# A pool of its own for the streamed matmul operands, at the upper end of on-chip memory

## The chip, the cores and the metric

The kernel runs on one core of one Trainium2 chip. The metric is the device time of one execution in microseconds (us); the lower the better. A core has a tensor engine (PE, with its weight loads shown apart as PEld), a vector engine (DVE), a scalar engine (ACT), GpSimd (POOL) and a synchronisation engine (SP) that here issues most of the transfers. Its on-chip memory has 128 partitions; in this program's allocation tiles lie between byte 16,384 and byte 229,376 of each partition.

## The reference

A sequence of 512 tokens with 1024 features goes through two blocks in float32.

```python
h = rms_norm(x, norm1_g);  z = h @ w_in
mix = concat([pool_mixer, gated short convolution, gated long convolution, differential attention])
x = x + mix @ w_out
h2 = rms_norm(x, norm2_g)
x = x + (silu(h2 @ w_gate) * (h2 @ w_up)) @ w_down
```

The second block puts 16 meta tokens in front and has two layers, each `h = h + layer(rms_norm_2(h, g))`: layer ab (sparse attention with a learned choice of keys, and a gated linear attention in chunks) and layer cd (a retention in chunks and a stick-breaking attention). A last norm ends it.

## The kernel before

Everything is kept transposed: features on the partitions, tokens along the free dimension. The activations are 8 tiles (kt) of 128 features by T = 528 columns, 16 meta tokens and 512 tokens. To reach float32 accuracy with faster matmuls, each operand is split into a high part and a low part (hi and lo) of the type float32r; a product is then three matmuls, hi by hi, lo by hi and hi by lo.

The work is staged as `run` (line 1342) has it: `setup`, `layer1` (line 394), `ffn` (646), `layer_ab` (772), `layer_cd` (1225). Each stage has a pool of its own ("l1", "ffn", "ab", "cd") that is closed at its end, so that the next stage's pool takes the same addresses; with `reuse_waits="tile"` a tile waits only for those earlier tiles that lay where it lies.

Three pools live through the whole kernel: "const" (line 63), "big" (64) and "w" (65). The pool "big" holds, among others, the residual x; `mx` (line 266, four tiles of 2 x 528 columns, 4,224 bytes each), in which mixed channels stand as hi and lo; and `hhi` and `hlo` (line 213, eight tiles each of 528 columns, 2,112 bytes), the hi and lo parts of the activations that `feed` (209) makes for each kt. The last stage also keeps its output weights in hhi and hlo (line 126). The pool "w" holds raw weights (`wraw`, two tiles of 4,096 bytes) and their parts (`whi`, `wlo`, four tiles each of 512 columns, 2,048 bytes).

`weights` (108) issues a weight load on SP's queue, casts it on ACT to hi (line 129) and subtracts on DVE to lo (line 130). `f_acc` (136) is the loop of nearly all matmuls: for each part of the contraction it issues three at line 144.

```python
for i, (ah, al) in enumerate(act):
    for j, (ww, aa) in enumerate(((wh, ah), (wh, al), (wl, ah))):
        nc.tensor.matmul(ps[b], lhsT=ww[i][:, f0:f0 + nf], rhs=aa[:, t0:t1], ...)
```

The operand `rhs` is streamed past the loaded weights. In layer 1 and in the gate and up projections of the FFN it is columns 16 to 528 of hhi and hlo; in the FFN's down projection it is `hidh` and `hidl` (lines 664 and 665, 13 tiles each of 512 columns, 2,048 bytes); in `add_out` (274) it is mx; in layers ab and cd it is mostly hhi and hlo in two parts of 272 and 256 columns. The FFN has two halves; each makes 11 tiles of hid by 22 products of 24 matmuls and then 8 outputs of 33 matmuls.

The order of the instructions on each engine comes from a scheduler that goes by priority: `first()` (73) raises it for loads and evictions, `chain()` (77) raises it further. The queues of transfers are in order: a transfer that waits holds up those behind it on its queue. Of layer ab, line 780 loads `gw2`, `sheared` (387) loads the attention bias `bh` on SP, and lines 862 and 1047 clear `avm`, `em` and `att` on POOL.

The program places the tiles at these bytes of a partition: x at 21,376; mx from 38,272; hhi from 57,280; hlo from 74,176; wraw from 96,000; whi from 104,192; wlo from 112,384; then, from 120,576, the stage pools: "l1" to 226,768, "ffn" to 186,112 (gu, sg, hidh from 132,864, hidl from 159,488), "ab" to 227,008, "cd" to 229,296. In ab, bh lies at 213,888.

Of the kernel before, what the change touches and what calls it, by code (L numbers as in the profile page):

```python
# [9 lines left out]
F32R = mybir.dt.float32r  # L10
# [10 lines left out]
T = S + M  # L21
H2 = M + S // 2
D = 1024
KT = 8
# [33 lines left out]
class Kern:  # L58
    def __init__(self, ctx, tc, io, dbg=None):
        self.tc, self.nc, self.io = tc, tc.nc, io  # L60
        self.dbg = dbg or {}
        E = ctx.enter_context
        self.const = E(tc.tile_pool(name="const", bufs=1))
        self.big = E(tc.tile_pool(name="big", bufs=1))
        self.wp = E(tc.tile_pool(name="w", bufs=2))
        self.dram = E(tc.tile_pool(name="dram", bufs=1, space=DRAM))
        self.ps = E(tc.tile_pool(name="ps", bufs=1, space=PSUM))
        self.wi = 0
        self.keep = False
        self.bg = []  # L70
# [37 lines left out]
    def weights(self, nk, ncol, cuts=1):  # L108

        if self.ahead:  # L110
            return self.ahead.pop()
        src = self.io["w"]
        n = nk * ncol
        out = [], []
        with self.first():
            raw = self.wp.tile([128, 1024], F32, name="wraw", bufs=2)
            for i in range(cuts):
                c = slice(i * n // cuts, (i + 1) * n // cuts)
                self.nc.sync.dma_start(raw[:, c], bass.AP(tensor=src.tensor, offset=src.offset + self.wi + c.start, ap=[[n, 128], [1, n // cuts]]))
            step = 512 // ncol  # L120
            for k0 in range(0, nk, step):
                k1 = min(k0 + step, nk)
                c = slice(k0 * ncol, k1 * ncol)
                w = c.stop - c.start
                if self.keep:
                    hi, lo = (self.big.tile([128, T], F32R, name=n, bufs=KT) for n in ("hhi", "hlo"))
                else:
                    hi, lo = (self.wp.tile([128, 512], F32R, name=n, bufs=4) for n in ("whi", "wlo"))
                self.nc.scalar.copy(hi[:, :w], raw[:, c])  # L129
                self.lo.tensor_tensor(out=lo[:, :w], in0=raw[:, c], in1=hi[:, :w].bitcast(F32), op=OP.subtract)  # L130
                for t, o in zip((hi, lo), out):
                    o += [t[:, k * ncol:(k + 1) * ncol] for k in range(k1 - k0)]
            self.wi += 128 * n
        return out
# [74 lines left out]
    def feed(self, kt, g, c0, c1, acc=None):  # L209

        nc = self.nc
        x = self.x[kt][:, c0:c1]
        hi = self.big.tile([128, T], F32R, name="hhi", bufs=KT)
        lo = self.big.tile([128, T], F32R, name="hlo", bufs=KT)
        g = self.cols[:, COLS[g][0] + kt:COLS[g][0] + kt + 1]
        nc.scalar.mul(hi[:, c0:c1], x, g)
        nc.vector.scalar_tensor_tensor(lo[:, c0:c1], x, g, hi[:, c0:c1].bitcast(F32), op0=OP.mult, op1=OP.subtract)  # L217
        if acc is not None:
            self.sumsq(kt, c0, c1, acc)
        return hi, lo  # L220
# [40 lines left out]
        return self.big.tile([128, T], F32, name="acc")  # L261

    def mx(self):
        return self.big.tile([128, 2, T], F32R, name="mx", bufs=4)

    def mix(self, src, c0, c1):

# [378 lines left out]
    def ffn(self, act, acc):  # L646
        nc, tc = self.nc, self.tc
        _, rb = self.norm(acc, False)
        rbx = rb[:, M:T]
        acc = self.newacc()  # L650
        out = [None] * 8
        with tc.tile_pool(name="ffn", bufs=1, reuse_waits="tile") as p:
            for half in range(2):
                hid = []
                for f in range(11):
                    t = p.tile([128, 2, S], F32, name="gu", bufs=2)
                    for g in range(2):
                        w = self.weights(8, 128)
                        ps = self.mm()
                        self.f_acc([ps], w, 0, 128, act, X)  # L660
                        with self.first():
                            nc.vector.tensor_tensor(out=t[:, g], in0=ps, in1=rbx, op=OP.mult)  # L662
                    sg = p.tile([128, S], F32, name="sg", bufs=2)
                    hi = p.tile([128, S], F32R, name="hidh", bufs=13)
                    lo = p.tile([128, S], F32R, name="hidl", bufs=13)
                    with self.first():
                        nc.scalar.activation(sg, t[:, 0], AF.Silu)
                        nc.vector.tensor_tensor(out=sg, in0=sg, in1=t[:, 1], op=OP.mult)
                        self.split(hi, lo, sg)
                    hid.append((hi, lo))  # L670
                if half == 1:
                    self.tables_ln()
                for o in range(8):
                    ps = self.mm()
                    for part, (k0, k1) in enumerate(((0, 6), (6, 11))):
                        w = self.weights(k1 - k0, 128)
                        self.f_acc([ps], w, 0, 128, hid[k0:k1], ((0, S),), part == 0, part == 1)
                    with self.first():
                        nc.vector.tensor_tensor(out=self.x[o][:, M:T], in0=self.x[o][:, M:T], in1=ps, op=OP.add)
                        if half == 1:  # L680
                            out[o] = self.feed(o, "ga", 0, T, acc)
        return out, acc
# [850 lines left out]
```

## Time and profile before

| | us |
|---|---|
| median of three runs | 1236.06 |
| lowest and highest of them | 1234.88, 1240.18 |
| the profiled execution, device time | 1235.71 |
| its span, first to last instruction | 1233.9 |

The profile is of one execution. "Busy" is the time in which an engine had an instruction in work; matmuls overlap one another by some 0.16 us, so their durations add up to more than the time they take, and the pace of a stream is read from the starts or from counts. The stages lie about so in the span: layer 1 to 216 us, the FFN to 578, layer ab to 929, layer cd to the end.

### The profile page before, as it was taken

Reading aid. Unit: us, or ns where it says so; the run is one execution under the profiler, and the core shown is the slowest. Engines: PE = TensorE matmul, PEld = TensorE weight load, DVE = VectorE, ACT = ScalarE, POOL = GpSimd, SP = SyncE. Lnnn points to the kernel's source line nnn. Section 1 sums busy time; section 2 is a strip of 40 time slices with the busy share of each in tenths; the row PEclk is TensorE's granted clock in tenths of the full one; section 3 lists DMA queues with packets and bytes.
Section 4 is the critical chain, followed back from the end, with each engine's and each line's share of the span. In section 5 each row is a group of like instructions: output and inputs, shape, how many; then the busy total and the mean of one; then the engine's idle time right before and its main releaser. Section 6 shows DMA issues by size and latency. Waiting matters only on the chain.

```text
span 1233.9 us, 19017 instructions
## 1 busy us (share of the span) xinstructions
PE 1208.5 (98%) x7246; PEld 1022.3 (83%) x7246; DVE 819.1 (66%) x1884; ACT 617.1 (50%) x1371; POOL 51.0 (4%) x60
## 2 busy tenths in 40 slices
PE   8999989999999999999999999999999999999996
PEld 5987767888888888888899899888899889876776
DVE  5899987444433444455699899765675575775775
ACT  5377645333322333344453445666553584575754
POOL 2100102000000000011000000000020000000000
PEclk9999999999999999999999999999999999999999
DMA  5421122232233322234222122222123213120122
GB/s 200 135 85 52 35 86 86 87 102 92 77 104 105 102 91 98 77 97 129 77 65 78 35 69 70 70 70 70 53 89 119 80 58 104 61 77 18 52 69 69
DMA packets 33111, 101.43 MB, mean 82 GB/s; under 512 B 4155, under 2 KB 6811, under 8 KB 33020
## 3 DMA queue, kind: packets, MB, share of 16 engines
q1 hardware_dynamic: 30236, 95.86, 24.4%
q0 software_dynamic: 976, 2.20, 0.7%
q10 hardware_dynamic: 1808, 2.16, 0.5%
q8 instruction: 57, 0.93, 0.3%
q14 instruction: 34, 0.28, 0.1%
HBM read 96.02 MB, written 3.10 MB: 80 GB/s over the span
## 4 chain that ended last, share of the span: by engine, by line
PE 87%; DVE 8%; ACT 2%; DMA 1%; issue 1%; POOL 0%; SPq 0%; DVEq 0%; POOLq 0%
PE mm L144 70%; PE psb L174 3%; DVE y L560 2%; DVE wlo L130 1%; PE pso L1217 1%; PE pso L970 1%; DVE sc L826 1%; PE psa L1098 1%; DVE m L825 1%; PE pso L972 1%; PE psa L1191 1%; DMA wraw<-in_w 1%; PE mm L163 1%; DMA relb<-in_relb 1%; PE psb L1191 0%
## 5 line engine op out<-in xcount | busy, mean ns | idle before, releaser
L144 PE MATMUL mm<-hhi,whi 128*128 128x512 f32 (+3 forms) x1296 | 442.6, 342 | 2.1 <-ACT whi L129 2.1
L144 PE MATMUL mm<-hhi,wlo 128*128 128x512 f32 (+3 forms) x1296 | 437.0, 337 | 0.2
L144 PE MATMUL mm<-hlo,whi 128*128 128x512 f32 (+3 forms) x1296 | 436.0, 336 | 0.2 <-DVE hlo L217 0.2
L129 ACT CAST whi<-wraw 128x512 fp32r<-128x512 f32 x350 | 207.8, 595 | 342.9 <-PE mm L144 311.5
L130 DVE TENSOR_TENSOR wlo<-wraw,whi 128x512 fp32r<-128x512 f32 x350 | 235.0, 674 | 156.3 <-ACT whi L129 128.8
L144 PEld LDWEIGHTS mm<-hhi,whi 128*128 128x128 f32 (+1 forms) x1296 | 245.2, 189 | 28.3 <-ACT whi L129 2.9
L144 PEld LDWEIGHTS mm<-hlo,whi 128*128 128x128 f32 (+1 forms) x1296 | 245.1, 189 | 26.6 <-issue 1.6
L144 PEld LDWEIGHTS mm<-hhi,wlo 128*128 128x128 f32 (+1 forms) x1296 | 244.8, 189 | 25.4 <-DVE wlo L130 1.0
L144 PE MATMUL mm<-mx,whi 128*128 128x512 f32 (+2 forms) x448 | 114.2, 343 | 3.3 <-ACT mx L102 3.1
L144 PEld LDWEIGHTS mm<-mx,whi 128*128 128x128 f32 x448 | 76.7, 192 | 15.6 <-ACT mx L102 3.7
L662 DVE TENSOR_TENSOR gu<-mm,rb 128x512 f32<-128x512 f32 x44 | 30.4, 692 | 71.2 <-PE mm L144 69.4
L144 PE MATMUL mm<-mx,wlo 128*128 128x512 f32 (+2 forms) x224 | 75.0, 335 | 0.0
L144 PE MATMUL mm<-hidh,whi 128*128 128x512 f32 x176 | 68.5, 389 | 0.0
L144 PE MATMUL mm<-hidh,wlo 128*128 128x512 f32 x176 | 68.5, 389 | 0.0
L144 PE MATMUL mm<-hidl,whi 128*128 128x512 f32 x176 | 68.5, 389 | 0.0
L231 POOL TENSOR_TENSOR acc<-acc,sq 128x528 f32<-128x528 f32 (+1 forms) x18 | 25.8, 1433 | 712.5 <-ACT sq L229 390.9
L300 DVE TENSOR_TENSOR tmp<-mm,rb 128x272 f32<-128x272 f32 (+2 forms) x76 | 35.7, 469 | 24.7 <-PE mm L144 23.7
L288 DVE TENSOR_TENSOR x<-x,mm 128x272 f32<-128x272 f32 (+2 forms) x72 | 36.7, 510 | 15.0 <-PE mm L144 13.8
L144 PEld LDWEIGHTS mm<-mx,wlo 128*128 128x128 f32 x224 | 42.7, 191 | 4.1 <-issue 0.2
L560 DVE SCALAR_TENSOR_TENSOR y<-u,cols,y 128x512 f32<-128x512 f32 x60 | 44.1, 760 | 0.2
L144 PEld LDWEIGHTS mm<-hidh,whi 128*128 128x128 f32 x176 | 33.0, 188 | 6.9
L144 PEld LDWEIGHTS mm<-hidh,wlo 128*128 128x128 f32 x176 | 33.0, 188 | 6.9
(398 smaller groups left out, 1793.2 us busy)
## 6 DMA issues: line engine op xcount, KB each, us to landing
wraw<-in_w SPq DMA_DIRECT2D x145, 512.0 KB, 3.5
wraw<-in_w SPq DMA_DIRECT2D x16, 384.0 KB, 3.0
wraw<-in_w SPq DMA_DIRECT2D x16, 320.0 KB, 2.8
bh<-tab SPq DMA_DIRECT2D x16, 132.0 KB, 2.8
mx<-cqk SPq DMA_DIRECT2D x8, 132.0 KB, 2.3
x<-in_x SPq DMA_DIRECT2D x4, 256.0 KB, 6.2
x<-in_x ACTq DMA_DIRECT2D x4, 256.0 KB, 5.4
B<-tab POOLq DMA_DIRECT2D x4, 256.0 KB, 5.3
```

Of the source, the lines that this page charges most:

```text
L129: self.nc.scalar.copy(hi[:, :w], raw[:, c])
L130: self.lo.tensor_tensor(out=lo[:, :w], in0=raw[:, c], in1=hi[:, :w].bitcast(F32), op=OP.subtract)
L144: nc.tensor.matmul(ps[b], lhsT=ww[i][:, f0:f0 + nf], rhs=aa[:, t0:t1], start=first and i == 0 and j == 0, stop=last and i == n - 1 and j == 2)
L163: nc.tensor.matmul(part(t), lhsT=aa[:, t0:t0 + nt], rhs=ww[i], start=u + i + j == 0 and t % 2 == 0, stop=u == 1 and i == 3 and j == 2, ski ...
L174: self.nc.tensor.transpose(out, in_, self.ident[:n, :n])
L231: e.tensor_tensor(out=acc[:, c0:c1], in0=acc[:, c0:c1], in1=sq[:, c0:c1], op=OP.add)
L288: nc.vector.tensor_tensor(out=x, in0=x, in1=p, op=OP.add)
L300: self.nc.vector.tensor_tensor(out=out[:, t0:t1], in0=p, in1=rb[:nf, t0:t1], op=OP.mult)
L560: nc.vector.scalar_tensor_tensor(y[:, f], u[:, f, k:k + S], cw[:, f, k:k + 1], y[:, f], op0=OP.mult, op1=OP.add)
L662: nc.vector.tensor_tensor(out=t[:, g], in0=ps, in1=rbx, op=OP.mult)
L825: nc.vector.max(out=m8, in_=sc)
L826: nc.vector.match_replace(out=sc, in_to_replace=m8, in_values=sc, imm_value=GONE)
```

## The change

mx, hhi and hlo go from the pool "big" into a new pool "hot" that is laid out from the upper end of the memory (`side="right"`); the FFN's pool is laid out from there downwards too, below "hot". Numbers of tiles, their sizes, the instructions and their operands stay as they are.

```diff
+        self.hot = E(tc.tile_pool(name="hot", bufs=1, side="right"))
...
-                    hi, lo = (self.big.tile([128, T], F32R, name=n, bufs=KT) for n in ("hhi", "hlo"))
+                    hi, lo = (self.hot.tile([128, T], F32R, name=n, bufs=KT) for n in ("hhi", "hlo"))
...
-        hi = self.big.tile([128, T], F32R, name="hhi", bufs=KT)
-        lo = self.big.tile([128, T], F32R, name="hlo", bufs=KT)
+        hi = self.hot.tile([128, T], F32R, name="hhi", bufs=KT)
+        lo = self.hot.tile([128, T], F32R, name="hlo", bufs=KT)
...
     def mx(self):
-        return self.big.tile([128, 2, T], F32R, name="mx", bufs=4)
+        return self.hot.tile([128, 2, T], F32R, name="mx", bufs=4)
...
-        with tc.tile_pool(name="ffn", bufs=1, reuse_waits="tile") as p:
+        with tc.tile_pool(name="ffn", bufs=1, reuse_waits="tile", side="right") as p:
```

## Rows read from the trace of the kernel before

**Rows 1.** The page: busy time of the engines, share of the span, instructions.
```profile
PE 1208.5 (98%) x7246; PEld 1022.3 (83%) x7246; DVE 819.1 (66%) x1884; ACT 617.1 (50%) x1371; POOL 51.0 (4%) x60
```

**Rows 2.** The page: the chain that ended last, by engine and by line.
```profile
PE 87%; DVE 8%; ACT 2%; DMA 1%; issue 1%; POOL 0%; SPq 0%; DVEq 0%; POOLq 0%
PE mm L144 70%; PE psb L174 3%; DVE y L560 2%; DVE wlo L130 1%; PE pso L1217 1%; PE pso L970 1%; DVE sc L826 1%; PE psa L1098 1%; DVE m L825 1%; PE pso L972 1%; PE psa L1191 1%; DMA wraw<-in_w 1%; PE mm L163 1%; DMA relb<-in_relb 1%; PE psb L1191 0%
```

**Rows 3.** Waits of PE: who waited for whom, us in total, times, longest.
```profile
PE mm L144 <- ACT mx L102: 3.1, 2, 2.9
```

**Rows 4.** Groups of instructions by shape, PE: busy us, mean ns, idle before.
```profile
L144 PE MATMUL mm<-hhi,whi 128*128 128x512 f32 x576 | 230.9, 402 | 2.1 <-ACT whi L129 2.1
...
L144 PE MATMUL mm<-hidh,whi 128*128 128x512 f32 x176 | 68.5, 389 | 0.0
...
L144 PE MATMUL mm<-mx,whi 128*128 128x512 f32 x192 | 64.9, 414 | 3.1 <-ACT mx L102 3.1
```

**Rows 5.** Busy time by stretch; stretch, length, engines, granted clock, DMA share, GB/s.
```profile
338.00:392.00 54.00, 54.00 (x240) 44.70 (x239) 18.59 (x36) 13.90 (x28) 0.00 (x0) 1.00 0.32 101
402.00:512.00 110.00, 110.00 (x478) 89.28 (x477) 52.05 (x80) 36.58 (x59) 0.00 (x0) 1.00 0.28 92
```

**Rows 6.** Timeline of PE at 333 us: start, duration, what.
```profile
333.03 0.40 PE L144 MATMUL mm<-hidh,whi 128*128 128x512 f32 x1
...
333.73 0.40 PE L144 MATMUL mm<-hidh,whi 128*128 128x512 f32 x1
...
335.12 0.39 PE L144 MATMUL mm<-hidh,whi 128*128 128x512 f32 x1
...
335.80 0.39 PE L144 MATMUL mm<-hidh,whi 128*128 128x512 f32 x1
```

**Rows 7.** Timeline of PE at 393 us.
```profile
392.92 0.39 PE L144 MATMUL mm<-hhi,whi 128*128 128x512 f32 x1
...
393.60 0.39 PE L144 MATMUL mm<-hhi,whi 128*128 128x512 f32 x1
...
394.30 0.39 PE L144 MATMUL mm<-hhi,whi 128*128 128x512 f32 x1
...
394.99 0.39 PE L144 MATMUL mm<-hhi,whi 128*128 128x512 f32 x1
...
395.68 0.40 PE L144 MATMUL mm<-hhi,whi 128*128 128x512 f32 x1
```

**Rows 8.** Tile gu: duration ns min/median/max, first and last start us.
```profile
L662 DVE TENSOR_TENSOR gu<-mm,rb x44: 691/692/692, 216.9 to 515.1; 128x512 f32<-128x512 f32 x44
```

**Rows 9.** Tile hidh: its last readers, its writers.
```profile
L144 PE MATMUL mm<-hidh,wlo x176: 389/389/397, 333.5 to 574.6; 128*128 128x512 f32 x176
L102 ACT CAST hidh<-sg x22: 620/621/621, 224.2 to 516.7; 128x512 fp32r<-128x512 f32 x22
```

**Rows 10.** Timeline of PE at 184 us; in brackets the idle time before.
```profile
184.46 2.38 PE L144 MATMUL mm<-mx,whi 128*128 128x512 f32 x4 [2.89 <-ACT mx L102]
```

**Rows 11.** Timeline of SP's queue at the end of the FFN.
```profile
573.73 0.36 SPq L391 DMA_DIRECT2D bh<-tab  x1
576.74 0.35 SPq L119 DMA_DIRECT2D wraw<-in_w  x1
```

**Rows 12.** The page: matmul groups, all shapes; hlo,whi and hhi,wlo have 1296, mx,wlo 224.
```profile
L144 PE MATMUL mm<-hhi,whi 128*128 128x512 f32 (+3 forms) x1296 | 442.6, 342 | 2.1 <-ACT whi L129 2.1
...
L144 PE MATMUL mm<-mx,whi 128*128 128x512 f32 (+2 forms) x448 | 114.2, 343 | 3.3 <-ACT mx L102 3.1
```

**Rows 13.** The page: weight loads, KB each, median us from issue to landing.
```profile
wraw<-in_w SPq DMA_DIRECT2D x145, 512.0 KB, 3.5
```

**Rows 14.** The page: the split of the weights, busy us, mean ns, idle before.
```profile
L129 ACT CAST whi<-wraw 128x512 fp32r<-128x512 f32 x350 | 207.8, 595 | 342.9 <-PE mm L144 311.5
L130 DVE TENSOR_TENSOR wlo<-wraw,whi 128x512 fp32r<-128x512 f32 x350 | 235.0, 674 | 156.3 <-ACT whi L129 128.8
```

**Rows 15.** Busy time in the stretch after the idle time of rows 10.
```profile
184.50:190.40 5.90, 5.90 (x13) 4.25 (x14) 3.98 (x5) 2.18 (x4) 0.94 (x1) 0.51 0.11 30
```

## The prediction, made before the change was run

> **What bounds the kernel now.** I read the page from the top. TensorE is busy for 1208.5 us of a span of 1233.9 us, VectorE for two thirds [rows 1]; the chain that ended last is PE for 87%, and one line, the matmul loop L144, for 70% [rows 2]. So the kernel is worth the number of its matmuls times their pace. The waits of TensorE say the same from the other side: the longest of them is 3.1 us in total [rows 3]. What is left to win or lose is the pace of the matmuls, or a new wait.
>
> The sum is made against the profiled execution: 1235.71 us, of which 1233.9 us is the span and 1.8 us lies around it. That is 0.35 us under the median of the three runs shown, 1236.06, so nothing need be scaled.
>
> **The pace, and what sets it.** The groups by shape show that matmuls of one shape do not all take the same: 128x512 fed from hhi last 402 ns on average, fed from hidh 389 ns, fed from mx 414 ns [rows 4]. A matmul starts before the one before it has ended, so I take the pace from counts. In a stretch that is all gate and up projection, 478 matmuls touch 110 us; one counts as soon as it overlaps the stretch, so the pace is (110 + 0.39) / 478 = 230.9 ns. In a stretch that is all down projection it is (54 + 0.39) / 240 = 226.6 ns [rows 5]. The clock is 1.00 (2.4 GHz) and PE fully busy in both.
>
> The streamed operand of the first kind lies low in memory (hhi from byte 57,344, hlo from 74,240), that of the second high (hidh from 132,864, hidl up to 186,112), and the weights of both lie between. So a reader might conclude that the upper end is faster, and this change puts hhi, hlo and mx there. Two places speak against it.
> - At 333.03 us the stream passes from hhi to hidh. The operands are high from there on, but the first step of three matmuls still takes 0.70 us and the next two 1.39, as with hhi; only from 335.12 on is it 0.68 [rows 6].
> - At 392.92 us it passes back. The first step reads hhi and hlo, low in memory, and takes 0.68 us; the next ones take 0.70, 0.69 and 0.69 [rows 7].
>
> What differs between the two kinds is not how high they lie but how they step. All hid tiles and all weight tiles are 2,048 bytes long and start at multiples of 256. The hhi and hlo tiles are 2,112 bytes long (528 columns), and are used in descending order of address, so each step of the contraction shifts the start of the streamed row by 64 bytes against the weights' grid: 0, 192, 128, 64, 0, and so on. A step takes 0.69 to 0.70 us, 692.8 ns on average (3 x 230.9), and 680 (3 x 226.6) where nothing shifts. I take that as the cause: place against the grid of 256 bytes, carried over from one matmul to the next.
>
> **The change part by part.**
> - Nothing is added or removed: the same matmuls, casts and transfers, 19,017 instructions before. Only addresses move, and with them which tiles of one stage lie on which tiles of another.
> - The new pool holds mx (4 x 4,224), hhi and hlo (8 x 2,112 each): 50,688 bytes, which is 198 x 256. If it ends at the top, 229,376, it begins at 178,688 with mx, then hhi at 195,584 and hlo at 212,480, all multiples of 256. All that lay above these tiles moves down by 50,688, so weights, hid and their grid keep their places modulo 256. The pitch of hhi and hlo stays 2,112; hi and lo of a step still have the same remainder; the eight starts still go through 0, 192, 128, 64. Only which step has which remainder is turned by one place. In a steady stream that is the same cycle: 1056 matmuls of the gate and up projections at 230.9 ns before and after. Term: 0.
> - The FFN's tiles: 65,536 bytes, so from 113,152 to 178,688, hid again at multiples of 256. 528 matmuls at 226.6 ns. Term: 0.
> - The other L144 matmuls (272 and 256 columns, and those fed from mx) have paces that no row separates by place. Bound from both sides: the largest difference seen for one shape, 4.3 ns, either way. For 960 more of 512 columns (from hhi and hlo 3 x 576 less 1,056, from mx 1.5 x 192 [rows 4]) that is 4.1 us, for the 2,544 narrower ones (4,560 from hhi, hlo and mx in all [rows 12], less 1,728 and 288) 10.9 us. I take 0, because of rows 6 and 7.
> - The FFN's tiles over those of layer 1. The first gu write is at 216.9 us [rows 8] and the first hid write at 224.2 [rows 9]. The layer 1 tiles that now lie under them (the bias, pooled and convolved channels, attention's exponentials) are last read by the mixes around the second add_out, whose first matmul starts at 184.46 us [rows 10]. The cover is over 25 us. Term: 0.
> - Layer ab over the FFN's tiles. Its first tiles (the gate weight gw, tmp, qk) no longer lie on FFN tiles, the later ones (the bias bh, the memsets of att, avm and em on POOL) now do: by my arithmetic bh lies on hidl. The last read of hid starts at 574.6 us and lasts 0.39 [rows 9], so it ends at 575.0. The first bh transfer was issued at 573.73 and will wait for that, 1.3 us; behind it on SP's queue is a weight load that was issued at 576.74 for another reason, its raw buffer [rows 11]. So nothing behind it is late. The memsets wait on POOL, which has 51 us of work in the whole span [rows 1]. Term: 0; if bh waited ahead of more loads, see the second rival.
> - cd ends 80 bytes below the new pool: it fits.
>
> Sum: 1235.7 + 0, and against the median 1236.0 us.
>
> On the pace, the row is that one shape has two paces at full clock, 230.9 and 226.6 ns [rows 5]. The Trainium skill, TensorE: Matmul & The Clock Gate, Part 2, Step-by-step, says that TensorE has two independent read ports, so that loading the next weights takes nothing from the running stream. By that rule place would not matter at all and the change would be worth 0; the trace does not agree with the premise, since place does matter here. By the row the change could be worth what the first rival gives.
>
> **The rivals.**
> - *The upper end is a different part of the memory, and a stream from there does not meet the weights.* For it: all fast matmuls read from above 131,072 in their steady state. Against it: rows 6 and 7. It would give 1056 x 4.3 = 4.6 us in the FFN, 4.1 us in the other wide ones, up to 10.9 in the narrow ones: about 1227 us, at most 1217.
> - *The queue at the FFN's end.* If the order on SP now has bh ahead of the weight loads that layer ab needs first, those wait for the last read of hid: issue at 575.0, landing 3.5 us later [rows 13], cast and subtraction 0.6 and 0.7 us [rows 14], ready at 579.8 where the first matmul of ab started right after the last of hid, at about 574.8. That is an idle of some 5 us. How much more it costs is seen at 184.46 us: after an idle of 2.89 us [rows 10] the granted clock is 0.51, the lower of its two levels (1.2 of 2.4 GHz), and 13 matmuls take 5.9 us [rows 15] in place of 13 x 0.231 = 3.0, so 2.9 us more. Together 7.9 us: 1244 us. It decides from the point at which the load stands behind bh. Against it: loads carry a higher priority than bh, and the issue at 576.74 is set by its buffer.
> - *The tiles stand in another order or off the grid in the new pool* (mirrored, say, so that the steps go up by 64 and not down). Then a step takes something between 680 and 700 ns, the ends of rows 6 and 7, instead of 692.8: for the 352 steps of gate and up -4.5 to +2.5 us, about double over the kernel, so 1227 to 1241; middle 1234.
>
> **How the numbers follow.** Forecast of no change, 1236.0: 0.57. Another order in the pool: 0.17, most of it still within 0.5%. Upper end faster: 0.15. Queue: 0.11. About 0.5% (6.2 us) is what a measurement here can tell from no change. Faster by more: the upper end's 0.15 and 0.03 of the third rival, 0.18. Slower: 0.10, nearly all of the queue's. Same: 0.72. The range goes from 1228, which takes in most of the other orders and the edge of the first rival, to 1241, some 5 us over the forecast, since the runs shown spread from 1234.88 to 1240.18 by themselves.
>
> **What would show it right or wrong.** Right: hhi-fed 128x512 matmuls still at 396 to 402 ns, hid-fed at 389, PE busy near 1208 us, and the bh issue after the last read of hid with the next load where it was. The first rival: all 128x512 at 389 and the gate and up stretch at 227 ns. The queue: an idle of PE near 575 us and a clock share under 1.00 in that slice. The third: a pace of gate and up other than 230.9 with hid's unchanged. Wrong altogether: hid's own pace changes, or a wait of PE on a tile of another stage.

## The result, and the profile after

The changed kernel is slower: a median of 1244.6 us (1237.9 to 1248.9, 20 runs) beside 1237.7 us (1232.7 to 1242.3, 20 runs) for the kernel before on the same chip, a ratio of 1.0057 with a 95% interval of 1.0039 to 1.0076. That is 6.8 us, just over the 0.5% named in the prediction, where no change was forecast. The profiled execution took 1245.0 us with a span of 1243.3.

The page of the changed kernel, busy time of the engines, answers to [rows 1]:

```profile
PE 1216.5 (98%) x7246; PEld 1024.5 (82%) x7246; DVE 819.0 (66%) x1884; ACT 617.6 (50%) x1371; POOL 51.5 (4%) x60
```

TensorE does the same 7246 matmuls and is busy 8.0 us longer; VectorE and ScalarE are where they were. So most of the time went into matmuls, not into waiting. The waits of PE in the changed kernel (who waited for whom, us in total, times, longest) agree; the first is that of [rows 3], 3.1 us in total in both, the second is 0.6 us longer than in [rows 4]:

```profile
PE mm L146 <- ACT mx L104: 3.1, 2, 2.8
PE mm L146 <- ACT whi L131: 2.7, 2, 1.7
```

(Line numbers are two higher than before; L146 is the loop of [rows 2].) Which matmuls? The groups by shape of the changed kernel (busy us, mean ns, idle before), for [rows 4]:

```profile
L146 PE MATMUL mm<-hhi,whi 128*128 128x512 f32 x576 | 231.4, 403 | 2.7 <-ACT whi L131 2.7
...
L146 PE MATMUL mm<-hidh,whi 128*128 128x512 f32 x176 | 69.6, 395 | 0.0
```

The matmuls fed from hidh went from 389 to 395 ns, those fed from hhi from 402 to 403. The stretches of the FFN say it as a pace (stretch, length, busy time and instructions of PE, PEld, DVE, ACT and POOL, granted clock, DMA share, GB/s), for [rows 5]:

```profile
341.00:395.00 54.00, 54.00 (x233) 43.45 (x233) 18.27 (x35) 13.79 (x29) 0.00 (x0) 1.00 0.32 100
407.00:517.00 110.00, 110.00 (x475) 88.94 (x474) 52.10 (x80) 36.54 (x59) 0.00 (x0) 1.00 0.27 91
```

By the prediction's formula the down projection runs at (54 + 0.39) / 233 = 233.4 ns a matmul, where it ran at 226.6, and gate and up at (110 + 0.39) / 475 = 232.4 ns, where it was 230.9. Clock 1.00, PE fully busy, as before. A count can be one off, which is 1.0 ns in the first and 0.5 ns in the second; the distances between starts in the trace give 233.3 against 226.7 (from the 13th matmul of each half on; the first twelve behind the passage of [rows 6] are slower before, so that all of a half come to 226.9) and 232.2 against 231.1. From the 13th matmul of gate and up (the first twelve start ahead of a short break in the stream) to the last of the down projection the starts say 366.90 us against 362.34: **4.56 us of the difference are in the FFN**, at full clock and with no new wait.

One row shows most of it. The tile hidh in the changed kernel (duration ns min/median/max, first and last start us), for [rows 9]:

```profile
L146 PE MATMUL mm<-hidh,wlo x176: 394/396/397, 336.9 to 582.0; 128*128 128x512 f32 x176
```

From the first such read to the last it is 245.1 us, and 574.6 - 333.5 = 241.1 before. This distance holds 528 matmuls of the down projection and 528 of gate and up.

The addresses tell why place had to be tried. They are read off the built program. In the changed kernel the tiles of the right side do not end at byte 229,376, the upper bound given ahead of the prediction, but at 229,344, 32 lower. So mx starts at 178,656, hhi at 195,552, hidh at 125,408 and hidl at 152,032: each first tile at remainder 224 modulo 256, while whi (53,504) and wlo (61,696), on the left side, are still at 0.

### The profile page after: what moved, and what is told of

Same layout as the page of the kernel before. It is cut to its first block, busy times and chain, and to the rows that moved or that the text cites. A ratio compares the mean times of both kernels' runs of the same rounds, so it can differ in the third digit from the quotient of the medians.

```text
span 1243.3 us, 19019 instructions
## 1 busy us (share of the span) xinstructions
PE 1216.5 (98%) x7246; PEld 1024.5 (82%) x7246; DVE 819.0 (66%) x1884; ACT 617.6 (50%) x1371; POOL 51.5 (4%) x60
## 4 chain that ended last, share of the span: by engine, by line
PE 87%; DVE 8%; ACT 2%; DMA 1%; issue 1%; POOL 0%; SPq 0%; DVEq 0%; POOLq 0%
PE mm L146 68%; PE psb L176 3%; PE mm L165 2%; PE pso L1219 1%; DVE wlo L132 1%; DVE sc L828 1%; PE pso L972 1%; DVE m L827 1%; DVE y L562 1%; PE psa L1100 1%; PE pso L974 1%; DMA wraw<-in_w 1%; ACT whi L131 1%; DVE qk L703 1%; PE psa L1193 1%
## 5 line engine op out<-in xcount | busy, mean ns | idle before, releaser
L146 PE MATMUL mm<-hhi,whi 128*128 128x512 f32 (+3 forms) x1296 | 443.1, 342 | 2.7 <-ACT whi L131 2.7
L146 PE MATMUL mm<-hhi,wlo 128*128 128x512 f32 (+3 forms) x1296 | 439.1, 339 | 0.2
L146 PE MATMUL mm<-hlo,whi 128*128 128x512 f32 (+3 forms) x1296 | 438.8, 339 | 0.0
L146 PEld LDWEIGHTS mm<-hhi,whi 128*128 128x128 f32 (+1 forms) x1296 | 246.5, 190 | 30.6 <-ACT whi L131 3.4
L146 PEld LDWEIGHTS mm<-hlo,whi 128*128 128x128 f32 (+1 forms) x1296 | 246.0, 190 | 26.7 <-issue 1.9
L146 PEld LDWEIGHTS mm<-hhi,wlo 128*128 128x128 f32 (+1 forms) x1296 | 245.4, 189 | 25.0 <-DVE wlo L132 1.0
L146 PE MATMUL mm<-mx,whi 128*128 128x512 f32 (+2 forms) x448 | 113.8, 342 | 3.9 <-ACT mx L104 3.1
L146 PEld LDWEIGHTS mm<-mx,whi 128*128 128x128 f32 x448 | 76.0, 190 | 16.4 <-ACT mx L104 3.7
L146 PE MATMUL mm<-mx,wlo 128*128 128x512 f32 (+2 forms) x224 | 74.9, 335 | 0.0
L146 PE MATMUL mm<-hidh,wlo 128*128 128x512 f32 x176 | 69.6, 396 | 0.0
L146 PE MATMUL mm<-hidh,whi 128*128 128x512 f32 x176 | 69.6, 395 | 0.0
L146 PE MATMUL mm<-hidl,whi 128*128 128x512 f32 x176 | 69.6, 395 | 0.0
L146 PEld LDWEIGHTS mm<-mx,wlo 128*128 128x128 f32 x224 | 42.6, 190 | 4.2 <-issue 0.2
L146 PEld LDWEIGHTS mm<-hidl,whi 128*128 128x128 f32 x176 | 33.1, 188 | 8.0
L146 PEld LDWEIGHTS mm<-hidh,wlo 128*128 128x128 f32 x176 | 33.1, 188 | 8.0
```

## The experiments

**Theory G**: the pace of a matmul of 512 columns is set by the remainder modulo 256 of the streamed row's start against that of the weights, and the change is slower because the right side ends 32 bytes lower. **Rival A**: the remainder of one of the two by itself. **Rival H**: the upper end, a new wait or a lower clock is what costs. None of the nine runs changes what is computed.

**1. Move only the weights.** They lie above nine small tiles; with these narrower, the weights, their raw tiles and the left-hand pools of the other stages move down by 288 bytes, and the streamed tiles stay.

```diff
--- the changed kernel
-        v = self.big.tile([128, 10], F32, name="rv", bufs=3)[:p, :w]
+        v = self.big.tile([128, 8], F32, name="rv", bufs=3)[:p, :w]
...
-        y, t = (self.big.tile([128, 10], F32, name=n, bufs=3)[:p, :w] for n in ("ry", "rt"))
+        y, t = (self.big.tile([128, 8], F32, name=n, bufs=3)[:p, :w] for n in ("ry", "rt"))
```

> The changed kernel with nine small tiles (rv, ry, rt) made 8 columns wide in place of 10, which moves the weight tiles down by 288 bytes: they now start at 224 modulo 256, as the streamed tiles of hid, which stay where they are, do. Theory G (the remainder of the streamed row against that of the weights sets the pace): down projection back at 226.6 ns a matmul (233.5 in the changed kernel), gate and up at 230.9 (232.1); time over that of the kernel before 1.000, between 0.998 and 1.002. Rival A (the remainder of the streamed row by itself, or of the weights by themselves, sets it): 233 ns stays or gets worse, ratio 1.005 or more. Rival H (the upper end of the memory is slower, or new waits or a slower clock made the difference): paces and ratio as in the changed kernel, 1.004 to 1.008.

Measured: ratio to before 1.0006 [0.9985, 1.0027]. Stretches of this kernel, down projection and gate and up:

```profile
340.00:394.00 54.00, 54.00 (x240) 44.73 (x239) 18.81 (x36) 13.90 (x28) 0.00 (x0) 1.00 0.32 100
406.00:516.00 110.00, 110.00 (x477) 89.33 (x476) 51.99 (x80) 37.25 (x60) 0.00 (x0) 1.00 0.29 92
```

240 and 477 matmuls where the changed kernel has 233 and 475: 226.6 ns and (110 + 0.39) / 477 = 231.4, the count of 478 of [rows 5] less one. The streamed tiles have not moved by a byte; the weights have, by 288 bytes, from 0 to 224 modulo 256. Rivals A and H both fall: hid at 224 runs at either pace, so it isn't the streamed row by itself, and weights at 0 do too (226.7 ns in the kernel before, 233.3 in the changed one), so it isn't the weights by themselves. It is the two places against one another that count, and the upper end is as fast as the lower. Beside it stands the rule that the prediction weighed: the Trainium skill, TensorE: Matmul & The Clock Gate, Part 2, Step-by-step, holds that the streamed operand and the weight load have a read port each, so that the one takes nothing from the other. Here a shift of the weights alone is worth 6.7 ns of each matmul of the down projection (233.3 to 226.7 by the starts), so for these streams the place of the weights does take something from the running matmul, and the measurement decides against the rule. That it is the weight load itself which meets the stream, and not another access to the weights, is what experiment 3 leaves.

**2. Put right side and weights at the remainders that the prediction had.**

```diff
--- the changed kernel, with the edit of experiment 1
+        E(tc.tile_pool(name="padl", bufs=1)).tile([128, 8], F32, name="padl")
         self.wp = E(tc.tile_pool(name="w", bufs=2))
+        E(tc.tile_pool(name="padr", bufs=1, side="right")).tile([128, 56], F32, name="padr")
         self.hot = E(tc.tile_pool(name="hot", bufs=1, side="right"))
```

> The changed kernel with a pad of 224 bytes on top of the new pool, the same nine tiles narrowed and a pad of 32 bytes below the weights: the streamed tiles lie at the upper end and at the remainders that the prediction took for granted (hid 0, weights 0, hhi and hlo multiples of 64). Theory G and rival A: down projection 226.6 ns, gate and up 230.9, ratio 1.000 (0.998 to 1.002). Rival H: 233 ns and 1.004 to 1.008.

Measured: ratio 1.0010 [0.9988, 1.0031]. The stretches:

```profile
341.00:395.00 54.00, 54.00 (x240) 44.70 (x239) 18.57 (x36) 13.90 (x28) 0.00 (x0) 1.00 0.32 101
407.00:517.00 110.00, 110.00 (x477) 89.37 (x476) 51.99 (x80) 37.24 (x60) 0.00 (x0) 1.00 0.28 92
```

With the pool's end at 229,120, a multiple of 256 as the prediction's 229,376 is, the paces are those of before, and the interval takes in no change. The terms of the prediction hold under its condition; the condition was wrong. The pads also hold height and grid apart: the streamed tiles lie as high as the changed kernel's, to 224 bytes.

**3. Take the kernel before, and put only the FFN's own tiles, hid among them, off the grid.** The others, gu and sg, are not read by TensorE.

```diff
--- the kernel before
         with tc.tile_pool(name="ffn", bufs=1, reuse_waits="tile") as p:
+            p.tile([128, 8], F32, name="pad")
             for half in range(2):
```

> The kernel before with one pad of 32 bytes ahead of the FFN's tiles: hid starts at 32 modulo 256, all else stays. Theory G and rival A: down projection about 233 ns in place of 226.6, 528 times, +3.4 us, gate and up unchanged at 230.9; ratio 1.003 (1.001 to 1.004). Rival H: 226.6 ns and 1.000.

Measured: ratio 1.0014 [0.9992, 1.0036]; with 3.4 us expected and an interval of about 2.7 us to either side, the time alone can't tell it from no change. The trace can. Stretches, and the tile hidh:

```profile
336.00:390.00 54.00, 54.00 (x233) 43.36 (x232) 18.19 (x36) 13.86 (x28) 0.00 (x0) 1.00 0.32 100
402.00:512.00 110.00, 110.00 (x477) 89.29 (x476) 51.87 (x80) 36.57 (x59) 0.00 (x0) 1.00 0.29 91
```

```profile
L144 PE MATMUL mm<-hidh,wlo x176: 392/395/397, 331.6 to 576.1; 128*128 128x512 f32 x176
```

The down projection has the changed kernel's 233 matmuls, gate and up have not moved, and the distance is 244.5 us, 3.4 more than before. Nothing else of the change is in this kernel, so the 32 bytes are enough for most of what the FFN lost.

This trace also tells what does not meet the stream. While the weights are cast and subtracted, ACT and DVE access the same tiles; but the matmuls are as slow where these engines do nothing. One such stretch, and starts of matmuls in it:

```profile
374.70:376.57 1.87, 1.87 (x10) 1.50 (x9) 0.00 (x0) 0.00 (x0) 0.00 (x0) 1.00 0.45 112
```

```profile
374.77 0.40 PE L144 MATMUL mm<-hidl,whi 128*128 128x512 f32 x1
...
375.47 0.39 PE L144 MATMUL mm<-hidl,whi 128*128 128x512 f32 x1
...
376.17 0.40 PE L144 MATMUL mm<-hidl,whi 128*128 128x512 f32 x1
```

A step of three still takes 0.70 us. In the two halves 80 distances between starts have no instruction of DVE, ACT or POOL within 0.3 us of them, and 151 no packet of a transfer; both come to 233.3 or 233.4 ns on average. So neither casts nor transfers make the pace, and PE's own weight loads are what is left.

**4. The changed kernel with the FFN's pool on the left.**

```diff
--- the changed kernel
-        with tc.tile_pool(name="ffn", bufs=1, reuse_waits="tile", side="right") as p:
+        with tc.tile_pool(name="ffn", bufs=1, reuse_waits="tile") as p:
```

> The changed kernel with the FFN's pool back on the lower side (hid at 0 modulo 256, hhi, hlo and mx 32 bytes off the grid as in the changed kernel). Theory G: down projection 226.6 ns, gate and up still 232, so 3.6 us of the changed kernel's 7 come back: ratio 1.003 (1.001 to 1.005). Rival A as G. Rival H: the down projection is as fast as in G if hid's height made it slow, with gate and up at 232; as slow as in the changed kernel if it did not (1.006).

Measured: ratio 1.0005 [0.9981, 1.0030], which holds both 1.000 and the expected 1.003. The stretches:

```profile
346.00:400.00 54.00, 54.00 (x240) 44.72 (x239) 18.62 (x36) 13.90 (x28) 0.00 (x0) 1.00 0.32 101
411.00:521.00 110.00, 110.00 (x475) 88.97 (x474) 51.49 (x79) 36.75 (x60) 0.00 (x0) 1.00 0.29 90
```

Down projection as before (240), gate and up as in the changed kernel (475). The FFN, again from the 13th matmul of gate and up to the last of the down projection, takes 363.44 us by the starts, 1.1 over before; experiment 3 has 365.76, 3.4 over. The two shares add up to 4.5, the changed kernel's 4.56.

**5 and 6. What each remainder costs.** One execution each of the kernel before, with hid at another place in each half of the FFN. With one time each (1241.6 and 1243.1 us) only the paces are read:

```diff
--- the kernel before (experiment 6 has 24 in place of 16)
             for half in range(2):
+                p.tile([128, 16], F32, name=f"pad{half}")
...
-                    hi = p.tile([128, S], F32R, name="hidh", bufs=13)
-                    lo = p.tile([128, S], F32R, name="hidl", bufs=13)
+                    hi = p.tile([128, S], F32R, name=f"hidh{half}", bufs=11)
+                    lo = p.tile([128, S], F32R, name=f"hidl{half}", bufs=11)
```

> The kernel before with hid at 64 modulo 256 against the weights in the first half of the FFN and at 128 in the second. Theory G1 (a change of the remainder from one step to the next costs, and a remainder that is no multiple of 64 costs): 226.7 ns in both halves. Theory G2 (each remainder has a price of its own, and only 0 is free): both halves between 228 and 234 ns, and not necessarily the same.

> As the run before, with hid at 96 modulo 256 in the first half and at 192 in the second. G1: 233.3 ns in the first half, as at 32 and at 224, and 226.7 in the second. G2: 233.3 in the first, over 228 in the second.

Down projections of the two halves, hid at 64 and at 128:

```profile
343.00:397.00 54.00, 54.00 (x238) 44.30 (x237) 18.59 (x36) 13.87 (x28) 0.00 (x0) 1.00 0.32 100
524.00:578.00 54.00, 54.00 (x234) 43.80 (x233) 25.76 (x43) 23.24 (x44) 8.08 (x6) 1.00 0.32 98
```

The same, hid at 96 and at 192:

```profile
340.00:394.00 54.00, 54.00 (x233) 43.46 (x232) 18.21 (x36) 13.87 (x28) 0.00 (x0) 1.00 0.32 100
523.00:577.00 54.00, 54.00 (x234) 43.48 (x233) 26.27 (x43) 22.67 (x43) 8.27 (x6) 1.00 0.33 101
```

By the starts of each half's 264 matmuls, from the 13th on: 228.9 ns at 64, 232.4 at 128, 233.3 at 192, 233.3 at 96, beside 226.7 at 0 and 233.3 at 32 and at 224. So G1 falls and G2 holds: a remainder has a price even where it never changes, and of the seven tried (160 was not) only 0 was free. The largest price, some 6.67 ns, is 16 cycles at 2.4 GHz.

These prices do not carry over to a stream that shifts. Their mean over 0, 64, 128 and 192 is 230.3, near the 231.1 of hhi, which goes through these four, but step by step they don't agree. In the kernel before, over the last 20 products of gate and up in the FFN's second half, a step of three matmuls takes 698.4 ns at 0, 698.3 at 192, 690.0 at 128 and 686.6 at 64, where by the fixed prices it would be 680, 700, 697 and 687. So the step at 0 is not free when it follows one at 64: as the prediction said, something is carried over from one matmul to the next. By what rule stays open.

**7. A version on the grid throughout the wide matmuls.** If the shifting pitch of hhi and hlo is what makes gate and up slower than the down projection, tiles of 2,048 bytes cure it. Layer 1 and the FFN don't need the 16 meta columns, so their hhi and hlo can be 512 columns; the products with tokens as rows count their tiles from column 0 too, and the pool is closed after the last gate and up projection and opened again with 528 columns.

```diff
--- the kernel before, with the pads and the narrow rv, ry, rt of experiment 2; mx stays in "big"
+        self.hotcm = tc.tile_pool(name="hot", bufs=1, side="right")
+        self.hot = self.hotcm.__enter__()
+        self.enter, self.W = E, S
...
-        hi = self.big.tile([128, T], F32R, name="hhi", bufs=KT)
-        lo = self.big.tile([128, T], F32R, name="hlo", bufs=KT)
+        hi = self.hot.tile([128, self.W], F32R, name="hhi", bufs=KT)
+        lo = self.hot.tile([128, self.W], F32R, name="hlo", bufs=KT)
+        o = T - self.W
...
-        nc.scalar.mul(hi[:, c0:c1], x, g)
+        nc.scalar.mul(hi[:, c0 - o:c1 - o], x, g)
...
-                        self.f_acc([ps], w, 0, 128, act, X)
+                        self.f_acc([ps], w, 0, 128, act, ((0, S),))
...
                     self.tables_ln()
+                    self.hotcm.__exit__(None, None, None)
+                    self.hot = self.enter(tc.tile_pool(name="hot2", bufs=1, reuse_waits="tile", side="right"))
+                    self.W = T
```

> The kernel before with hhi and hlo in a pool at the upper end, with a pad on top so that it is on the weights' grid, and with tiles of 512 columns (2,048 bytes) for layer 1 and the FFN, where the 16 meta columns are not needed; for the layers ab and cd the pool is reopened with tiles of 528 columns. Nothing else of the computation changes. Theory G: gate and up take 226.7 ns a matmul like the down projection, in place of 231.1, 1056 times, so 4.7 us less; the 288 products of layer 1 as well, 1.3 us; ratio 0.995 (0.993 to 0.998). Rival L (gate and up are slower than the down projection because each of its products waits for a load of new weights or an eviction more often, not because of place): 231 ns and 1.000. Rival H (height): 231 ns or more and 1.000 to 1.004.

Measured: 1233.6 us, ratio 0.9977 [0.9958, 0.9997]. The stretches:

```profile
336.00:390.00 54.00, 54.00 (x240) 44.74 (x239) 18.52 (x35) 13.90 (x28) 0.00 (x0) 1.00 0.33 101
398.00:508.00 110.00, 110.00 (x487) 91.11 (x486) 51.55 (x80) 37.26 (x61) 0.00 (x0) 1.00 0.29 94
```

Gate and up now have 487 matmuls in 110 us, (110 + 0.39) / 487 = 226.7 ns, the pace of the down projection, with as many weight loads and evictions per product as ever. Rival L falls, and H once more: these rows are read from above byte 196,000. Nor are the first steps of hid slow any more, as they were in [rows 6]: all of a half's 264 matmuls come to 226.7 ns. Between the same two matmuls the FFN takes 357.72 us by the starts, 4.62 less than before.

**8 and 9. Both once more, side by side.** The time of experiment 7 fell by 2.9 us where its paces fell by 5.3 (4.6 in the FFN; layer 1's 288 wide products of hhi and hlo went from 231.8 to 229.3 ns, 0.7 us). The profile of the changed kernel showed the last matmul 8.9 us later, more than its paces explain. So both were timed again on one chip.

> The kernel with tiles of 2,048 bytes for layer 1 and the FFN once more, beside the changed kernel on the same chip. If the paces are all there is (4.6 us in the FFN, about 0.7 us in layer 1's 288 products), 5.3 us less than before, ratio 0.9957; if some of it is given back elsewhere, nearer to the 0.9977 of the first measurement.

> The changed kernel itself on the same chip. If the paces are all there is (4.6 us in the FFN, 0.6 to 0.7 us each in layer 1's 288 products and in its 288 matmuls fed from mx, nothing in the narrow matmuls), 5.9 us more than before, ratio 1.0048 (1.003 to 1.007). If the slower start and the lower clock of its one profile belong to the change, 8.8 us, 1.007.

Measured: the kernel of experiment 7 1232.7 us, ratio 0.9961 [0.9943, 0.9980]; the changed kernel 1242.2 us, ratio 1.0041 [1.0020, 1.0062]. Both agree with the paces alone (0.9957 and 1.0048), and 1.007 lies outside this interval, though not outside that of the first measurement (1.0039 to 1.0076). In the second profile of the changed kernel the FFN's stretches have the same counts:

```profile
340.00:394.00 54.00, 54.00 (x233) 43.48 (x232) 18.27 (x35) 13.78 (x29) 0.00 (x0) 1.00 0.31 95
405.00:515.00 110.00, 110.00 (x475) 88.97 (x474) 51.61 (x79) 36.73 (x59) 0.00 (x0) 1.00 0.29 93
```

**The rest of the difference between the first two profiles** (spans of 1243.3 and 1233.9 us, 9.4 apart; less the FFN's 4.56, 4.8) is mostly not shown to be the change. The kernel before and experiments 3, 5 and 6 have the same layer 1 at the same addresses, yet their first read of hid by this line comes at 333.5, 331.6, 338.5 and 335.5 us: 6.9 us apart. The granted clock differs. First 50 us of the changed kernel, and 650 to 670 us:

```profile
0.00:50.00 50.00, 44.92 (x190) 33.87 (x191) 30.74 (x67) 24.94 (x45) 13.00 (x29) 0.90 0.59 184
650.00:670.00 20.00, 19.96 (x124) 17.64 (x123) 16.22 (x49) 9.02 (x18) 0.00 (x0) 0.83 0.17 57
```

Of experiment 3 (hid at 32):

```profile
0.00:50.00 50.00, 45.75 (x223) 35.68 (x224) 34.71 (x74) 26.12 (x47) 12.81 (x29) 1.00 0.61 189
650.00:670.00 20.00, 20.00 (x157) 18.92 (x156) 18.87 (x59) 8.10 (x15) 0.00 (x0) 1.00 0.27 80
```

Of experiment 6 (hid at 96 and 192):

```profile
650.00:670.00 20.00, 20.00 (x123) 17.70 (x123) 16.10 (x48) 8.54 (x17) 0.00 (x0) 0.83 0.15 53
```

Of the changed kernel once more, in experiment 9:

```profile
650.00:670.00 20.00, 19.96 (x149) 18.06 (x149) 19.05 (x59) 9.88 (x21) 0.00 (x0) 1.00 0.21 73
```

The dip to 0.83 that the changed kernel's first profile shows at 650 us is there in experiment 6 too, whose layer ab lies exactly as before, and is not there in the changed kernel's second profile. One profile of each kernel can't be subtracted outside the stretches at full clock.

## Why the prediction was wrong

- **What bounds the kernel: right.** The pace of the matmuls, not a wait; the whole difference that could be assigned is pace at full clock.
- **What sets the pace: right in part.** Place against the weights' grid of 256 bytes, not height, as rows 6 and 7 were read; experiments 1 and 2 show it, and moving the weights alone does the same as moving the stream. Wrong was "What differs between the two kinds is not how high they lie but how they step", with 680 ns a step "where nothing shifts": in experiments 3, 5 and 6 nothing shifts from step to step, and a step takes up to 700. By that reading hid would have kept its pace wherever the pool ended.
- **The step that failed: "If it ends at the top, 229,376, it begins at 178,688 ... all multiples of 256", and from it "hid again at multiples of 256 ... 528 matmuls at 226.6 ns. Term: 0."** The right side ends at 229,344, so hid lay 32 bytes off the weights' grid and ran at 233.3: 528 x 6.67 = 3.5 us, 3.4 measured in experiment 3. The condition was written down, and the term was summed as if it held.
- **hhi and hlo, "In a steady stream that is the same cycle": wrong for the same reason.** The four remainders became 224, 32, 96 and 160, and the pace 232.2 for 231.1: 1056 x 1.1 = 1.2 us by the starts, 1.1 in experiment 4.
- **The other wide matmuls, taken as 0 between bounds of 4.3 ns either way:** by the intervals between starts at full clock, those fed from mx went from 230.3 to 232.7 ns in layer 1 (192 of them) and from 230.7 to 233.3 in the last stage (96, together 0.7 us), layer 1's fed from hhi and hlo from 231.8 to 232.7 (288, 0.3 us), and those of layers ab and cd from 231.6 to 232.4 (384, 0.3 us). The narrow ones, where the bound was 10.9 us, gave nothing: 125.4 ns before and after at 272 columns, 118.7 and 118.3 at 256. With the FFN's 4.56 this is 5.9 us, inside both intervals (4.8 to 9.4 us and 2.5 to 7.7). The forecast of 1236.0 us itself rests on three runs; the median of 20 for the kernel before is 1.7 us higher.
- **Layer 1's cover and the queue at the FFN's end: right.** SP's queue in the changed kernel, where bh goes out 0.23 us after the last read of hid has started and the weight load behind it 1.9 us later, for [rows 11]:

```profile
580.46 0.42 SPq L782 DMA_DIRECT2D gw<-in_gw  x1
582.19 0.33 SPq L393 DMA_DIRECT2D bh<-tab  x1
584.08 0.35 SPq L121 DMA_DIRECT2D wraw<-in_w  x1
```

  The last matmul from hid starts at 581.96 and the first of layer ab at 582.19, one pace later, with no idle time. The second rival did not come.
- **The first rival, that the upper end is faster:** false. hid at 125,184 and up in experiment 2 and at 82,176 in experiment 4 runs at the same 226.7 ns, and hhi, streamed from above 195,000 in experiment 2, at the 231.1 that it had low in memory. (In its sum, 1056 x 4.3 is 4.5 and not 4.6 us, and its end 1216, not 1217.)
- **The third rival had the mechanism ("off the grid") but the wrong bounds.** It let a step of three matmuls take 680 to 700 ns, the ends of rows 6 and 7, and this held: 3 x 233.3 = 700. But it applied this to gate and up only, where it ends at +2.5 us, and left hid at its 680. hid had the most to lose, since it stood on the one remainder found free. With hid from 680 to 700 the rival's upper end would have been 176 x 0.02 = 3.5 us higher, 1244 to 1245.

## What to carry to other kernels

When a stream of wide matmuls is bound by its own pace, look at the start addresses of streamed rows and weights in the built program, and at the pitch of the tiles: on the weights' grid the matmul of 512 columns took 226.7 ns here, off it up to 233.3, and tiles without the 64 spare bytes made the whole kernel 0.2 to 0.4% faster (0.9977 and 0.9961). That the sizes of tiles are multiples of the grid does not make it free to move them: where the region begins or ends decides, and it is read off the allocation, not assumed. And a difference of a few us that lies in layer 1 here must be read with the granted clock beside it, or from counts in stretches at 1.00.

## What had not been expected of the hardware

The price hangs on the streamed row and the weights together: with both at remainder 224 the pace is that of both at 0. In experiment 2 hidh minus whi is 71,936 = 281 x 256, an odd multiple, and still fast, so a distance that is an odd multiple of 256 is free too. The prices are 2.2 ns at 64, 5.7 at 128 and 6.7 at 32, 96, 192 and 224; matmuls of 272 and 256 columns differ by no more than 0.4 ns between the kernel before and the changed one. No run has them on the grid throughout, so whether they would gain there was not tried. That the weight loads are what meets the stream is left by exclusion (experiment 3) and was not varied by itself.
